# Decoder step on one core: norm factors spread inside the second product, second weight sum one block later, activations last in a step, smaller first transfers

## The chip, the core and the metric

The kernel runs on one core of a Trainium2 chip. The metric is device microseconds (us) of one execution. The engines of the core work side by side, each through its own list of instructions in order: TensorE (PE, matrix products, results in PSUM), VectorE (DVE), ScalarE (ACT), GpSimd (POOL), and SyncE (SP), which here mostly issues DMA transfers. An engine waits at an instruction until the semaphores that it names have come, and everything behind that instruction on the same engine waits too.

## What is computed

One layer of a decoder over T = 576 token columns (512 of a prompt, 64 of eight running sequences), model width 1024. The part that the change touches is the pair of half-step feed-forward networks and the norms around them:

```
def _rmsnorm(x, g):
    y = xf * lax.rsqrt(jnp.mean(xf * xf, axis=-1, keepdims=True) + EPS)
    return (y * g.astype(jnp.float32)).astype(x.dtype)

def _swiglu(h, w_up, w_down):
    a, g = jnp.split(h @ w_up, 2, axis=-1)
    return (jax.nn.silu(g) * a) @ w_down

    x = x + 0.5 * _swiglu(_rmsnorm(x, W['g_ffn1'][l]), W['w_ffn1_up'][l], W['w_ffn1_down'][l])
    mix, ... = _mixer(_rmsnorm(x, W['g_mix'][l]), ...)
    x = x + mix
    x = x + 0.5 * _swiglu(_rmsnorm(x, W['g_ffn2'][l]), W['w_ffn2_up'][l], W['w_ffn2_down'][l])
y = _rmsnorm(x, W['g_final'])
```

The hidden width is 2816, that is 22 blocks ("features" f = 0 to 21) of 128. The mixer between the two networks (mLSTM and GLA, merged by gates) starts from a product of the normed input with `w_in`, taken as a list of tiles of 128 output channels.

## The kernel before

**Number format.** Every large product is made of three passes over split operands, hi·xh, hi·xl and lo·xh. For each weight ACT writes the rounded upper part (`whi`), and DVE subtracts it from the weight (`wlo`). In the same way an activation gets its `xh` and `xl`, or `mh` and `ml`. Activations stand with channels on partitions and the 576 tokens along the row, cut into two halves of 288. A matmul is 128x128 by 128x288.

**Norms.** The channel gain is multiplied in at the split. The factor of each token comes later, at the results, which are multiplied with a tile `r` of 128x576. `Norm.start` adds the squares over partitions (PE), takes the root (ACT) and the reciprocal (DVE, line 245). `Norm.finish` spreads these factors to all partitions by 4 to 8 small matmuls (line 255) and copies them to `r` (ACT). The first product of the second network and of the mixer's input runs on the unscaled input. `start` is called from inside that first product (the list `midway`), and `finish` is called behind the second product. The PSUM pool `pd` of the large products has two buffers, so the third product can start only when the first has been read out by an operation that needs `r`.

**A feed-forward network (`ffn`).** Features 0 and 1 are plain: two products of 48 matmuls each. Features 2 to 21 are made by a scheme with seven products in place of eight: the weight is cut into four quarters A11, A12, A21, A22 (128x512 each), four sums of them are built (S1 = A21 + A22 and S2 = S1 - A11 on DVE, S3 and S4 on POOL), the input has its four sums T1 to T4 (`combine`: tiles `xt`, `xth`, `xtl`), and the blocks A11, S2, A12, S3, S1, A22, S4 of 12 matmuls each run one after the other. Between the blocks of a feature stand blocks "d" of the down product of the features before. The results are put together on ACT and DVE: `s` (copy of A11's result), `U2` and `U3` (sums, in the rows `U`), then the two halves of `t` (gate) and of `h` (value), SiLU on ACT, `h·t`, and the split `mh`/`ml`.

**Order.** This stretch is in an order written out by hand. `blocks` lists all blocks. After the matmuls of a block a step is emitted: first the `prep` events (ACT, `whi` of the block four ahead), then the posts that `later(d, ...)` has put d steps ahead (the work on the results), then the other events: weight loads, weight sums, and `prep_lo` (DVE, `wlo`). A group of four features has 9 or 11 steps per feature. A PSUM tile `pd` holds A11's and then A12's result in one half, and S1's and then S4's in the other. So block S1 must wait for the DVE operation that reads A12's half for `t` (line 408), and block S4 for the one that reads S1's result into `h` (line 410).

**Start and end.** The head (lines 502 to 549) loads the first weights and inputs in pieces on SP's queue and makes the first two products together, k by k. The last norm goes by token halves. `Norm.square` puts the square of each of the eight channel tiles on ACT, POOL adds them up in `acc`, and PE adds `acc` and the last square over partitions (`packed_sum`, line 156).

Helpers hide callers in the profile: L54 is any two-operand operation, L57 one with a scalar, L66 any activation, L122 the products of `dense`, L423 all blocks of the hand-written order.

Of the kernel before, what the change touches and what calls it, by code (L numbers as in the profile page):

```python
# [9 lines left out]
F32 = mybir.dt.float32  # L10
F32R = mybir.dt.float32r
# [4 lines left out]
P = 128  # L16
# [21 lines left out]
def step_kernel(ctx: ExitStack, tc: tile.TileContext, a):  # L38
# [75 lines left out]
    def mm3(ps, w, parts, nk, hfs):  # L114

        hi, lo = w
        for k in range(nk):
            if k == nk // 2 and midway:
                midway.pop()()
            for n, (wt, xt) in enumerate(((hi, parts[k][0]), (hi, parts[k][1]), (lo, parts[k][0]))):  # L120
                for hf in hfs:
                    nc.tensor.matmul(  # L122
                        ps[:, hf, :HALF], lhsT=wt[:, k, :], rhs=xt[:, hf * HALF:(hf + 1) * HALF],
                        start=(k == 0 and n == 0), stop=(k == nk - 1 and n == 2),
                    )
# [38 lines left out]
    class Norm:  # L164
# [11 lines left out]
        def square(self, k, s=slice(0, T)):  # L176
            n = s.stop - s.start
            acc = self.acc.setdefault(s.start, [])
# [68 lines left out]
        def finish(self, keep=True):  # L247
# [3 lines left out]
            r = xs.tile([P, 4 * n], F32, name="r", tag="r", bufs=1) if keep else None  # L251
# [10 lines left out]
    def ffn(x, norm, wup, wdn, fp, after, head=None, parts=((0, 1),)):  # L262

# [13 lines left out]
        for f in range(PLAIN):  # L277
# [30 lines left out]
        NAMES = ("A11", "S2", "A12", "S3", "S1", "A22", "S4")  # L308
        XOF = {"A11": "B11", "S2": "T2", "A12": "B21", "S3": "T3", "S1": "T1", "A22": "T4", "S4": "B22"}
        first = [0] + list(range(PLAIN, NF, GRP))  # L310
        size = [PLAIN] + [GRP] * (len(first) - 1)
        blocks, at_f = [], {}
        for g in range(1, len(first)):
            last = g == len(first) - 1
            o = 0
            for j in range(size[g]):
                f = first[g] + j
                at_f[f] = len(blocks)
                blocks += [(f, n) for n in NAMES]
# [6 lines left out]
        raw, parts_of, posts = {}, {}, {}  # L326
        pair = [None]
        tick = [0]

        def prep(i):  # L330

            b = blocks[i]
            if i % 2 == 0:
                pair[0] = [wp.tile([P, KT, P], F32R, name=f"w{n}", tag=f"w{n}", bufs=3) for n in ("hi", "lo")]
            if b[0] == "d":
                n = size[b[1]]
                src = raw["d"][b[1:]]
            else:
                n = 4
                src = raw[b[0]][b[1]]  # L340
            hi, lo = (t[:, 4 * (i % 2):4 * (i % 2) + n, :] for t in pair[0])
            act(hi, src, AF.Copy)
            parts_of[i] = hi, lo, src

        def prep_lo(i):
            hi, lo, src = parts_of[i]
            tt(lo, src, hi, ALU.subtract)
            parts_of[i] = hi, lo

        def load_up(f):  # L350
            st = wp.tile([P, 2, 4, P], F32, name="wst", tag="wst", bufs=3)
            su = fp.tile([P, 2, 4, P], F32, name="wsu", tag="wsu", bufs=2)
            for i, t in ((1, su), (0, st)):
                nc.sync.dma_start(out=t, in_=wup[f, :, i].rearrange("p (h k) c -> p h k c", h=2))
            raw[f] = {"A11": st[:, 0], "A12": st[:, 1], "A21": su[:, 0], "A22": su[:, 1]}

        def load_down(i):

            raw.setdefault("d", {})
            st = wp.tile([P, KT, P], F32, name="wst", tag="wst", bufs=3)  # L360
            _, g, o, hfs = blocks[i]
            n = size[g]
            sv_ = st[:, :2 * n, :].rearrange("p (o k) c -> p o k c", o=2)
            nc.sync.dma_start(out=sv_, in_=wdn[o:o + 2, :, first[g]:first[g] + n].rearrange("o p k c -> p o k c"))
            for u in range(2):
                raw["d"][(g, o + u, hfs)] = sv_[:, u]

        def sums(f, *names):
            w = raw[f]
            for n in names:  # L370
                a, b, op, eng = {"S1": ("A21", "A22", ALU.add, None), "S2": ("S1", "A11", ALU.subtract, None),
                                 "S3": ("A11", "A21", ALU.subtract, nc.gpsimd),
                                 "S4": ("A12", "S2", ALU.subtract, nc.gpsimd)}[n]
                w[n] = fp.tile([P, 4, P], F32, name=n, tag=n, bufs=1)
                tt(w[n], w[a], w[b], op, eng=eng)

        events = {}

        def on(i, fn, *a_):
            events.setdefault(i, []).append((fn, a_))  # L380

        for f, i in at_f.items():
            on(i - 11, load_up, f)
            on(i - 5, sums, f, "S1", "S2")
            on(i - 4, sums, f, "S3")
            on(i - 2, sums, f, "S4")
        for i, b in enumerate(blocks):
            if b[0] == "d" and b[2] % 2 == 0:
                on(i - 8, load_down, i)
            on(i - 4, prep, i)  # L390
            on(i - 4, prep_lo, i)

        def later(d, fn):
            posts.setdefault(tick[0] + d, []).append(fn)

        def seven(f, psum, lastf):
# [3 lines left out]
            s1, U2, U3 = (fp.tile([P, HALF], F32, name=n, tag=n, bufs=1) for n in ("s1", "U2", "U3"))  # L400
            t1, t2, h1, h2, r2 = t[:, :HALF], t[:, HALF:], h[:, :HALF], h[:, HALF:], r[:, HALF:]
# [4 lines left out]
            later(1, lambda: act(s1, psum["A11"], AF.Copy))  # L406
            later(2, lambda: tt(U2, psum["S2"], s1, ALU.add))
            later(3, lambda: tt(t1, psum["A11"], r[:, :HALF], ALU.mult))
            later(4, lambda: tt(U3, psum["S3"], U2, ALU.add))
            later(5, lambda: tt(h2, psum["S1"], U3, ALU.add))  # L410
            later(6, lambda: tt(h1, psum["A22"], U3, ALU.add))
            later(7, lambda: tt(t2, psum["S1"], U2, ALU.add))
            later(7, lambda: tt(t2, t2, r2, ALU.mult, eng=pool_))
# [6 lines left out]
        def run(i, work):  # L420

            for m in work:
                nc.tensor.matmul(m[0], lhsT=m[1], rhs=m[2], start=m[3], stop=m[4], skip_group_check=m[5])  # L423
            do = events.pop(i, ())
            for fn, a_ in do:
                if fn is prep:
                    fn(*a_)
            for fn in posts.pop(tick[0], ()):
                fn()
            for fn, a_ in do:  # L430
                if fn is not prep:
                    fn(*a_)
            tick[0] += 1

        with tc.manual_schedule():
            for i in range(min(events), 0):
                for fn, a_ in events.pop(i, ()):
                    fn(*a_)
            psum = {}
            for i, b in enumerate(blocks):  # L440
                if b[0] == "d":
                    _, g, o, hfs = b
                    n = size[g]
                    hi, lo = parts_of.pop(i)
                    ps = pd.tile([P, 2, 512], F32, name="pd", tag="pd")
                    work = [(ps[:, hf, :HALF], wt[:, k, :], xt[:, hf * HALF:(hf + 1) * HALF],
                             k == 0 and m == 0, k == n - 1 and m == 2, False)
                            for k in range(n) for m, (wt, xt) in enumerate(
                                ((hi, mids[g][k][0]), (hi, mids[g][k][1]), (lo, mids[g][k][0]))) for hf in hfs]
                    half = 12 if len(work) > 12 else len(work)  # L450
                    run(i, work[:half])
                    if midway:
                        midway.pop()()
                    if work[half:]:
                        run(i, work[half:])

                    def done(ps=ps, o=o, hfs=hfs, fin=g == len(first) - 1):
                        s_ = slice(hfs[0], hfs[-1] + 1)
                        stt(halves(x[o])[:, s_], ps[:, s_, :HALF], 0.5, ALU.mult, halves(x[o])[:, s_], ALU.add)
                        if fin:  # L460
                            later(1, lambda: after(o, hfs))
                    later(0, done)
                    continue
                f, n = b
                if n == "A11":
                    if (f - PLAIN) % GRP == 0:
                        mids.append([])
# [877 lines left out]
```

## Time and profile before

| | |
|---|---|
| median of 3 runs | 1604.49 us (1599.73 to 1606.45) |
| profiled execution | 1603.93 us, of which the span from first to last instruction is 1602.1 us |
| PE busy | 1563.5 us, 98% |
| DVE busy | 1061.5 us, 66% |
| ACT busy | 678.4 us, 42% |
| POOL busy | 310.0 us, 19% |
| DMA | 166.01 MB, mean 104 GB/s |
| mean granted TensorE clock | 0.996 |

The busy times are shares of one execution. A PE at 98% can get shorter only by the time in which it stands still or runs at the lower of its two clock levels, or by fewer matmuls. In rows of the trace, the first number is the start in us from the span's start, the second the duration. A bracket at the end is the idle time of that engine just before the row, and what ended it.

### The profile page before, as it was taken

What the parts mean: (1) busy time and instruction counts of PE and PEld (TensorE: products, weight loads), DVE (VectorE), ACT (ScalarE), POOL (GpSimd) and SP (SyncE); (2) the same over time, 40 slices, a digit from 0 to 9 for tenths busy, and PEclk for the clock granted to TensorE, in tenths of its full rate; (3) what the DMA queues carried; (4) which work ended last, traced back from release to release, by engine and by line L of the source; (5) the groups of instructions that cost most, each with busy time, mean ns of one, the idle gap of its engine ahead of it and who ended that gap; (6) DMA issues with size and microseconds to landing.
All of it is one profiled execution on the core that took longest, in us unless ns stands there. A gap on an engine that the chain in (4) does not pass through costs nothing.

```text
span 1602.1 us, 31170 instructions
## 1 busy us (share of the span) xinstructions
PE 1563.5 (98%) x13028; PEld 1514.5 (95%) x13028; DVE 1061.5 (66%) x1785; ACT 678.4 (42%) x1147; POOL 310.0 (19%) x300
## 2 busy tenths in 40 slices
PE   8999999999999999999999999999999999999997
PEld 7999999999998989999998989999999999999997
DVE  7986776767587666653565756633567977677775
ACT  8433433333555453631334344531453433333334
POOL 1333223321200000000100001003223422322223
PEclk9999999999999999999999999999999999999999
DMA  5222332233513313323432334442222232223223
GB/s 188 82 96 80 94 93 91 80 92 95 189 54 123 110 48 116 112 94 114 129 136 90 132 108 153 152 158 79 80 93 66 83 102 93 79 81 105 93 66 112
DMA packets 59332, 166.01 MB, mean 104 GB/s; under 512 B 6072, under 2 KB 14008, under 8 KB 58168
## 3 DMA queue, kind: packets, MB, share of 16 engines
q1 hardware_dynamic: 58616, 163.43, 31.8%
q8 instruction: 103, 1.69, 0.4%
q10 hardware_dynamic: 576, 0.59, 0.1%
q14 instruction: 37, 0.30, 0.1%
HBM read 142.60 MB, written 21.38 MB: 102 GB/s over the span
## 4 chain that ended last, share of the span: by engine, by line
PE 87%; DVE 6%; ACT 3%; issue 2%; POOL 1%; DMA 0%; SPq 0%; ACTq 0%; DVEq 0%; POOLq 0%
PE pd L122 36%; PE pd L423 32%; PE pm L423 10%; ACT whi L66 1%; DVE wlo L54 1%; PE pm L1075 1%; PE pm L794 1%; PE pd L533 1%; PE pm L1089 1%; PE pm L869 1%; DVE xt L57 1%; DVE ml L54 1%; PE pm L1141 1%; PE pm L722 1%; DVE xtl L54 0%
## 5 line engine op out<-in xcount | busy, mean ns | idle before, releaser
L66 ACT ACTIVATE whi<-wst 128x512 fp32r<-128x512 f32 (+3 forms) x301 | 217.9, 736 | 448.0 <-PE pd L122 271.8
L54 DVE TENSOR_TENSOR wlo<-wst,whi 128x512 fp32r<-128x512 f32 (+3 forms) x301 | 262.0, 871 | 22.4 <-ACT whi L66 15.1
L122 PE MATMUL pd<-xh,whi 128*128 128x288 f32 x1136 | 249.2, 298 | 5.4 <-DVE t L54 3.5
L122 PE MATMUL pd<-xh,wlo 128*128 128x288 f32 x1136 | 247.6, 296 | 0.0
L122 PE MATMUL pd<-xl,whi 128*128 128x288 f32 x1136 | 247.4, 297 | 0.0
L122 PEld LDWEIGHTS pd<-xh,whi 128*128 128x128 f32 x1136 | 182.8, 188 | 10.4 <-issue 9.7
L54 POOL TENSOR_TENSOR t<-t,r 128x288 f32<-128x288 f32 (+1 forms) x80 | 105.2, 1315 | 445.6 <-DVE t L54 399.6
L66 ACT ACTIVATE whi<-S 128x512 fp32r<-128x512 f32 x160 | 99.7, 626 | 208.9 <-PE pd L423 74.8
L122 PEld LDWEIGHTS pd<-xh,wlo 128*128 128x128 f32 x1136 | 183.5, 189 | 1.9 <-issue 1.8
L122 PEld LDWEIGHTS pd<-xl,whi 128*128 128x128 f32 x1136 | 182.6, 188 | 1.4 <-issue 1.0
L57 DVE SCALAR_TENSOR_TENSOR x<-pd,x 128x576 f32<-128x576 f32 (+1 forms) x112 | 79.8, 713 | 142.9 <-PE pd L423 116.8
L423 PE MATMUL pd<-mh,whi 128*128 128x288 f32 x704 | 156.3, 296 | 0.3 <-DVE x L57 0.3
L423 PE MATMUL pd<-mh,wlo 128*128 128x288 f32 x704 | 155.9, 296 | 0.0
L423 PE MATMUL pd<-ml,whi 128*128 128x288 f32 x704 | 155.9, 296 | 0.0
L423 PE MATMUL pd<-xh,whi 128*128 128x288 f32 x480 | 144.4, 301 | 7.5 <-DVE h L54 3.0
L423 PE MATMUL pm<-xth,wlo 128*128 128x288 f32 x480 | 141.9, 296 | 0.9 <-DVE wlo L54 0.9
L423 PE MATMUL pd<-xh,wlo 128*128 128x288 f32 x480 | 142.4, 297 | 0.0
L423 PE MATMUL pd<-xl,whi 128*128 128x288 f32 x480 | 142.3, 296 | 0.0
L423 PE MATMUL pm<-xth,whi 128*128 128x288 f32 x480 | 141.9, 296 | 0.0
L423 PE MATMUL pm<-xtl,whi 128*128 128x288 f32 x480 | 141.8, 296 | 0.0
L54 DVE TENSOR_TENSOR wlo<-S,whi 128x512 fp32r<-128x512 f32 x160 | 126.5, 791 | 0.6
L423 PEld LDWEIGHTS pd<-mh,whi 128*128 128x128 f32 x704 | 114.9, 189 | 0.7 <-DVE x L57 0.5
(318 smaller groups left out, 3227.9 us busy)
## 6 DMA issues: line engine op xcount, KB each, us to landing
wst<-in_win SPq DMA_DIRECT2D x65, 512.0 KB, 3.7
wst<-in_wup SPq DMA_DIRECT2D x46, 512.0 KB, 4.8
wst<-in_wdn SPq DMA_DIRECT2D x44, 512.0 KB, 3.7
wsu<-in_wup SPq DMA_DIRECT2D x40, 512.0 KB, 4.0
C<-in_C SPq DMA_DIRECT2D x16, 514.0 KB, 5.0
out_Cs<-C SPq DMA_DIRECT2D x16, 514.0 KB, 3.1
S<-in_S SPq DMA_DIRECT2D x4, 1024.0 KB, 4.9
out_Ss<-S SPq DMA_DIRECT2D x4, 1024.0 KB, 4.1
```

The costliest lines, as they stand in the source:

```text
L54: (eng or nc.vector).tensor_tensor(out=out, in0=in0, in1=in1, op=op)
L57: nc.vector.scalar_tensor_tensor(out=out, in0=in0, scalar=s, in1=in1, op0=op0, op1=op1)
L66: nc.scalar.activation(out=out, in_=in_, func=func, **kw)
L122: nc.tensor.matmul(ps[:, hf, :HALF], lhsT=wt[:, k, :], rhs=xt[:, hf * HALF:(hf + 1) * HALF], start=(k == 0 and n == 0), stop=(k == nk - 1 ...
L423: nc.tensor.matmul(m[0], lhsT=m[1], rhs=m[2], start=m[3], stop=m[4], skip_group_check=m[5])
L533: nc.tensor.matmul(ps[i][:, hf, :HALF], lhsT=wt[:, k, :], rhs=xt[:, hf * HALF:(hf + 1) * HALF], start=(k == 0 and n == 0), stop=(k == KT - ...
L722: nc.tensor.transpose(out=pt[:, c, j * P:(j + 1) * P], in_=src[j][:, (c0 + c) * P:(c0 + c + 1) * P], identity=ident)
L794: nc.tensor.matmul(po[32 * g:32 * g + 32, :], lhsT=qpad(b_)[j], rhs=states(b_)[j], start=(v == 0 and j == 0), stop=False)
L869: nc.tensor.matmul(pl[32 * g:32 * g + 32, c, :], lhsT=kk[:, o:o + 32], rhs=qq[:, o:o + 32], start=True, stop=True)
L1075: nc.tensor.matmul(pc, lhsT=ktok[:, c, j * P:(j + 1) * P], rhs=vtok[:, c, :], start=True, stop=True)
L1089: nc.tensor.matmul(po[:, c, :], lhsT=Cc[c - 1][:, d, es], rhs=qs[d][:, c * P:(c + 1) * P], start=False, stop=(d == 1))
L1141: nc.tensor.matmul(pu, lhsT=kb[:, b_ // 4, b_ % 4, j * P:(j + 1) * P], rhs=vb[:, b_ // 4, :], start=True, stop=True)
```

## The change

Five edits, and a move of code. The hand-written pipeline goes from inside `ffn` into the functions `pipeline` and `unite` beside it, with the same blocks and the same `later` distances; the diff below leaves that move out.

```
 def mm3(ps, w, parts, nk, hfs):
             if k == nk // 2 and midway:
-                midway.pop()()
+                midway.pop(0)()
 def square(self, k, s=slice(0, T)):
+            last = KT - 1 if n == T else KT - 2
-            if k == 0 or k == KT - 1:
+            if k == 0 or k >= last:
                 acc.append(sq)
 def ffn(...):
                 if f == 0:
                     midway.append(norm.start)
                 pg = up(f, 0)
+                if f == 0:
+                    midway.append(norm.finish)
                 pa = up(f, 1)
                 if f == 0:
-                    r = norm.finish()
+                    r = norm.r
-            on(i - 5, sums, f, "S1", "S2")
-            on(i - 4, sums, f, "S3")
+                on(i - 5, sums, b[0], "S1")
+                on(i - 4, sums, b[0], "S2", "S3")
-            later(e[2], lambda: tt(h, h, t, ALU.mult))
+            later(e[2], lambda: tt(h, h, t, ALU.mult), not lastf)
             later(e[3], lambda: act(hi, h, AF.Copy))
-            later(e[3], lambda: tt(lo, h, hi, ALU.subtract))
+            later(e[3], lambda: tt(lo, h, hi, ALU.subtract), not lastf)
+        def later(d, fn, last=False):
+            posts.setdefault(tick[0] + d, []).append((last, fn))
 def run(i, work):
-            for fn in posts.pop(tick[0], ()):
-                fn()
+            late = posts.pop(tick[0], ())
+            for last, fn in late:
+                if not last:
+                    fn()
             for fn, a_ in do:
                 if fn is not prep:
                     fn(*a_)
+            for last, fn in late:
+                if last:
+                    fn()
-        load_w(0, 2)
-        load(0, 1)
-        load_w(2, 5)
+        load_w(0, 1)
+        load(0)
+        load_w(1, 3)
+        load(1)
+        load_w(3, 5)
         midway.append(n2.start)
-        first = [win_tile(), win_tile()]
-        r = n2.finish()
+        first = [win_tile()]
+        midway.append(n2.finish)
+        first.append(win_tile())
+        r = n2.r
```

Three places show how instructions move. The first is DVE in the first network, around features 5 and 6 (before, then after). `U_1246` (after: `U_1254`) is U3 of feature 5, `S_1336` and `S_1338` (after: `S_1341` and `S_1360`) are the sums S1 and S2 of feature 6, and `h<-pd` is the read of S1's result that block S4 waits for.

```order
L54 TENSOR_TENSOR h<-h,t 128x576
L54 TENSOR_TENSOR t<-pd,r 128x288
L54 TENSOR_TENSOR wlo<-wst,whi 128x512
L54 TENSOR_TENSOR ml<-h,mh 128x576
L54 TENSOR_TENSOR U_1246<-pm,U_1245 128x288
L54 TENSOR_TENSOR S_1336<-wsu 128x512
L54 TENSOR_TENSOR S_1338<-S_1336,wst 128x512
L54 TENSOR_TENSOR wlo<-wst,whi 128x512
L54 TENSOR_TENSOR h<-pd,U_1246 128x288
```

```order
L54 TENSOR_TENSOR t<-pd,r 128x288
L54 TENSOR_TENSOR wlo<-wst,whi 128x512
L54 TENSOR_TENSOR h<-h,t 128x576
L54 TENSOR_TENSOR U_1254<-pm,U_1253 128x288
L54 TENSOR_TENSOR S_1341<-wsu 128x512
L54 TENSOR_TENSOR wlo<-wst,whi 128x512
L54 TENSOR_TENSOR ml<-h,mh 128x576
L54 TENSOR_TENSOR h<-pd,U_1254 128x288
L54 TENSOR_TENSOR S_1360<-S_1341,wst 128x512
```

The split `ml` has moved from ahead of U3 to behind S1 and `wlo`, `h·t` behind `t` and `wlo`, and the sum S2 from ahead of `h<-pd` to behind it.

The second place is DVE in the second network's start, around the read of its first product into `t` (before, then after).

```order
L57 SCALAR_TENSOR_TENSOR xt<-x_11968,sm,xg 128x288
L57 SCALAR_TENSOR_TENSOR xt<-x_11968,sm,xt 128x288
L54 TENSOR_TENSOR wlo<-wst,whi 128x1024
L54 TENSOR_TENSOR xtl<-xt,xth 128x576 x2
L54 TENSOR_TENSOR t<-pd,r 128x576
L54 TENSOR_TENSOR S_13806<-wsu 128x512
```

```order
L57 SCALAR_TENSOR_TENSOR xt<-x_11974,sm,xg 128x288
L57 SCALAR_TENSOR_TENSOR xt<-x_11974,sm,xt 128x288
L54 TENSOR_TENSOR xtl<-xt,xth 128x576
L54 TENSOR_TENSOR t<-pd,r 128x576
L54 TENSOR_TENSOR xtl<-xt,xth 128x576
L54 TENSOR_TENSOR wlo<-wst,whi 128x1024
L54 TENSOR_TENSOR S_13812<-wsu 128x512
```

The read `t` now stands behind one `xtl` instead of behind `wlo` and two `xtl`.

The third place is DVE at the mixer's first tiles. `G` is the read of the first tile (gates), `Gs` its split copy that the gate products use, `kTg` the read of the third tile.

```order
L54 TENSOR_TENSOR wlo<-wst,whi 128x1024
L54 TENSOR_TENSOR G<-pd,r 128x576
L57 SCALAR_TENSOR_TENSOR qTg<-pd,r 128x576
L54 TENSOR_TENSOR Gs<-G,Gs 16x576
L54 TENSOR_TENSOR kTg<-pd,r 128x576
```

```order
L54 TENSOR_TENSOR G<-pd,r 128x576
L54 TENSOR_TENSOR Gs<-G,Gs 16x576
L57 SCALAR_TENSOR_TENSOR qTg<-pd,r 128x576
L54 TENSOR_TENSOR wlo<-wst,whi 128x1024
L54 TENSOR_TENSOR kTg<-pd,r 128x576
```

`G` now stands ahead of the `wlo` of the next tile, and `Gs` ahead of `qTg`. On PE the four spreading matmuls stand in the middle of the second tile's 48 matmuls instead of behind them.

## Rows read from the trace of the kernel before

**Rows 1.** The page, busy time of each engine.

```profile
PE 1563.5 (98%) x13028; PEld 1514.5 (95%) x13028; DVE 1061.5 (66%) x1785; ACT 678.4 (42%) x1147; POOL 310.0 (19%) x300
```

**Rows 2.** Waits of PE: line, releaser, us in total, times, longest.

```profile
PE pd L423 <- DVE h L54: 3.0, 4, 1.3
PE pd L423 <- ACT whi L66: 2.9, 4, 0.8
PE pd L423 <- DVE t L54: 2.0, 13, 0.2
```

**Rows 3.** Stretches: length, each engine's busy time, granted clock, DMA.

```profile
49.27:390.00 340.73, 336.63 (x2501) 332.74 (x2501) 254.79 (x415) 131.22 (x235) 100.78 (x75) 1.00 0.29 90
1216.88:1563.00 346.12, 341.99 (x2545) 338.11 (x2544) 258.99 (x421) 134.13 (x241) 100.89 (x75) 1.00 0.28 88
124.33:141.88 17.55, 17.55 (x134) 17.55 (x134) 13.23 (x22) 7.22 (x13) 5.18 (x4) 1.00 0.29 91
433.00:446.00 13.00, 13.00 (x96) 12.77 (x97) 2.04 (x3) 11.67 (x23) 0.00 (x0) 1.00 0.14 42
1202.94:1206.36 3.42, 3.42 (x16) 3.42 (x16) 2.86 (x3) 0.69 (x2) 2.68 (x2) 0.50 0.00 0
```

**Rows 4.** Timeline of DVE at a feature of the 11-step kind, 144 to 150 us.

```profile
144.66 0.76 DVE L54 TENSOR_TENSOR ml<-h,mh 128x576 fp32r<-128x576 f32 x1 [1.72 <-ACT mh L66]
...
146.30 0.45 DVE L54 TENSOR_TENSOR t<-pd,r 128x288 f32<-128x288 f32 x1
...
148.36 0.69 DVE L54 TENSOR_TENSOR S<-S,wst 128x512 f32<-128x512 f32 x1
```

**Rows 5.** Timeline of PE at the same place.

```profile
146.37 0.29 PE L423 MATMUL pm<-xth,wlo 128*128 128x288 f32 x1
146.81 0.40 PE L423 MATMUL pd<-xth,whi 128*128 128x288 f32 x1 [0.15 <-DVE t L54]
```

**Rows 6.** Timelines of DVE and PE between features 5 and 6.

```profile
110.94 0.76 DVE L54 TENSOR_TENSOR ml<-h,mh 128x576 fp32r<-128x576 f32 x1 [0.64 <-ACT mh L66]
...
113.91 0.45 DVE L54 TENSOR_TENSOR h<-pd,U 128x288 f32<-128x288 f32 x1
...
114.51 0.37 PE L423 MATMUL pd<-xh,whi 128*128 128x288 f32 x1 [1.30 <-DVE h L54]
```

**Rows 7.** Timelines of PE and DVE at the mixer's first tiles.

```profile
429.94 1.14 PE L255 MATMUL pm<-v,cst 128*128 128x144 f32 x8
433.00 0.50 PE L122 MATMUL pd<-xh,whi 128*128 128x288 f32 x2 [1.92 <-DVE G L54]
...
432.11 0.75 DVE L54 TENSOR_TENSOR G<-pd,r 128x576 f32<-128x576 f32 x1
```

**Rows 8.** Timelines of PE and DVE at the second network's start.

```profile
1202.42 0.50 PE L122 MATMUL pd<-xh,whi 128*128 128x288 f32 x2 [3.49 <-DVE t L54]
...
1199.06 1.21 DVE L54 TENSOR_TENSOR wlo<-wst,whi 128x1024 fp32r<-128x1024 f32 x1
...
1201.53 0.74 DVE L54 TENSOR_TENSOR t<-pd,r 128x576 f32<-128x576 f32 x1
```

**Rows 9.** Timelines of ACT, POOL and PE at the end.

```profile
1591.40 0.44 ACT L66 ACTIVATE sq<-x 128x288 f32<-128x288 f32 x1 [1.15 <-DVE x L57]
...
1592.02 0.79 POOL L54 TENSOR_TENSOR acc<-acc,sq 128x288 f32<-128x288 f32 x1
...
1592.86 0.36 PE L156 MATMUL pm<-acc,cst 128*32 128x72 f32 x8 [2.05 <-POOL acc L54]
```

**Rows 10.** Timeline of PE, its first matmuls.

```profile
6.58 1.09 PE L533 MATMUL pd<-xh,whi 128*128 128x288 f32 x3 [6.58 <-ACT xh L66]
```

**Rows 11.** Timelines of DVE and POOL where both run, and POOL's pause.

```profile
105.05 1.92 DVE L54 TENSOR_TENSOR wlo<-wsu,whi 128x512 fp32r<-128x512 f32 x1
...
104.52 1.89 POOL L54 TENSOR_TENSOR t<-t,r 128x576 f32<-128x576 f32 x1 [1.22 <-ACT t L66]
...
152.56 1.19 POOL L54 TENSOR_TENSOR t<-t,r 128x288 f32<-128x288 f32 x1 [12.29 <-DVE t L54]
```

More of the change, by code (lines that the diff above doesn't have):

```diff
@@ L250, in finish @@
             per = 2 if n == T // 4 else 4
-            r = xs.tile([P, 4 * n], F32, name="r", tag="r", bufs=1) if keep else None
+            self.r = r = xs.tile([P, 4 * n], F32, name="r", tag="r", bufs=1) if keep else None
             for i in range(4 // per):
@@ L260, in finish, with unite @@
             return r
+    NAMES = ("A11", "S2", "A12", "S3", "S1", "A22", "S4")
+    XOF = {"A11": "B11", "S2": "T2", "A12": "B21", "S3": "T3", "S1": "T1", "A22": "T4", "S4": "B22"}
+    def unite(psum, t, h, r, fp, later):
+        s1, U2, U3 = (fp.tile([P, HALF], F32, name=n, tag=n, bufs=1) for n in ("s1", "U2", "U3"))
+        later(1, lambda: act(s1, psum["A11"], AF.Copy))
+        later(2, lambda: tt(U2, psum["S2"], s1, ALU.add))
+        later(3, lambda: tt(t[:, :HALF], psum["A11"], r[:, :HALF], ALU.mult))
+        later(4, lambda: tt(U3, psum["S3"], U2, ALU.add))
+        later(5, lambda: tt(h[:, HALF:], psum["S1"], U3, ALU.add))
+        later(6, lambda: tt(h[:, :HALF], psum["A22"], U3, ALU.add))
+        later(7, lambda: tt(t[:, HALF:], psum["S1"], U2, ALU.add))
@@ L304, in ffn @@
             mids[0].append((hi, lo))
-        NAMES = ("A11", "S2", "A12", "S3", "S1", "A22", "S4")
-        XOF = {"A11": "B11", "S2": "T2", "A12": "B21", "S3": "T3", "S1": "T1", "A22": "T4", "S4": "B22"}
         first = [0] + list(range(PLAIN, NF, GRP))
         size = [PLAIN] + [GRP] * (len(first) - 1)
-        blocks, at_f = [], {}
+        blocks = []
         for g in range(1, len(first)):
@@ L316, in ffn @@
             for j in range(size[g]):
-                f = first[g] + j
-                at_f[f] = len(blocks)
-                blocks += [(f, n) for n in NAMES]
+                blocks += [(first[g] + j, n) for n in NAMES]
                 for _ in range(1 if last and j >= GRP - 2 else 2):
@@ L324, in ffn @@
         blocks += [("d", len(first) - 1, o, hfs) for hfs in parts for o in range(KT)]
[L326 to L383, printed above, removed]
-            on(i - 5, sums, f, "S1", "S2")
-            on(i - 4, sums, f, "S3")
[L386 to L394, printed above, removed]
@@ L396, in seven, with up_done @@
-        def seven(f, psum, lastf):
+        def up_done(f, psum, later):
+            if (f - PLAIN) % GRP == 0:
+                mids.append([])
             t = fp.tile([P, T], F32, name="t", tag="t", bufs=2)
             h = fp.tile([P, T], F32, name="h", tag="h", bufs=2)
-            s1, U2, U3 = (fp.tile([P, HALF], F32, name=n, tag=n, bufs=1) for n in ("s1", "U2", "U3"))
-            t1, t2, h1, h2, r2 = t[:, :HALF], t[:, HALF:], h[:, :HALF], h[:, HALF:], r[:, HALF:]
+            lastf = f == NF - 1
@@ L405, in seven @@
             e = (8, 9, 9, 10) if lastf else (9, 9, 12, 13)
[L406 to L412, printed above, removed]
@@ L413, in seven @@
-            later(7, lambda: tt(t2, t2, r2, ALU.mult, eng=pool_))
+            unite(psum, t, h, r, fp, later)
+            later(7, lambda: tt(t[:, HALF:], t[:, HALF:], r[:, HALF:], ALU.mult, eng=pool_))
             later(e[0], lambda: act(t, t, AF.Silu))
             later(e[1], lambda: tt(t, t, r, ALU.mult, eng=pool_))
-            later(e[2], lambda: tt(h, h, t, ALU.mult))
+            later(e[2], lambda: tt(h, h, t, ALU.mult), not lastf)
             later(e[3], lambda: act(hi, h, AF.Copy))
-            later(e[3], lambda: tt(lo, h, hi, ALU.subtract))
@@ L420, in run @@
[L420 to L427, printed above, removed]
-            for fn in posts.pop(tick[0], ()):
-                fn()
[L430 to L467, printed above, removed]
-                    pair_ = pd.tile([P, 2, 512], F32, name="pd", tag="pd")
-                    psum = {"A11": pair_[:, 0, :HALF], "S1": pair_[:, 1, :HALF]}
-                    psum["A12"], psum["S4"] = psum["A11"], psum["S1"]
-                    seven(f, psum, f == NF - 1)
-                if n not in psum:
-                    psum[n] = bank([P, HALF], "b" + n)
-                hi, lo = parts_of.pop(i)
-                go_on = n in ("A12", "S4")
-                run(i, [(psum[n], wt[:, k, :], xt, not go_on and k == 0 and m == 0, k == 3 and m == 2, go_on)
-                        for k, (xh, xl) in enumerate(norm.block(XOF[n]))
-                        for m, (wt, xt) in enumerate(((hi, xh), (hi, xl), (lo, xh)))])
-            while posts:
-                for fn in posts.pop(min(posts)):
-                    fn()
@@ new lines, in up_done, with down_work @@
+            later(e[3], lambda: tt(lo, h, hi, ALU.subtract), not lastf)
+        def down_work(b, w, ps):
+            _, g, o, hfs = b
+            n = size[g]
+            hi, lo = w
+            return [(ps[:, hf, :HALF], wt[:, k, :], xt[:, hf * HALF:(hf + 1) * HALF],
+                     k == 0 and m == 0, k == n - 1 and m == 2, False)
+                    for k in range(n) for m, (wt, xt) in enumerate(
+                        ((hi, mids[g][k][0]), (hi, mids[g][k][1]), (lo, mids[g][k][0]))) for hf in hfs]
@@ new lines, in down_done @@
+        def down_done(b, ps, later):
+            _, g, o, hfs = b
+            s_ = slice(hfs[0], hfs[-1] + 1)
+            stt(halves(x[o])[:, s_], ps[:, s_, :HALF], 0.5, ALU.mult, halves(x[o])[:, s_], ALU.add)
+            if g == len(first) - 1:
+                later(1, lambda: after(o, hfs))
+        pipeline(blocks, norm, fp, lambda f, i: wup[f, :, i], up_done,
+                 (lambda b: size[b[1]], lambda b: wdn[b[2]:b[2] + 2, :, first[b[1]]:first[b[1]] + size[b[1]]],
+                  down_work, down_done))
```

100 lines of the change are left out of this document (added).

## The prediction

> **What bounds the kernel now.** I read the busy times first. PE is busy 1563.5 us, 98% of the span, and no other engine more than two thirds [rows 1]. So the end is set by PE, and this change, which takes no product away, can only win the places where PE stands still or runs at the lower clock level. The view of PE's waits says where these are inside the hand-written order: 4 waits for `h`, 4 that are put down to `whi`, 13 short ones for `t`, 7.9 us in all [rows 2]. Then I looked at stretches. Between 124.33 and 141.88 PE runs without a stop: two of the 134 matmuls there belong to the piece before, and 132 in 17.55 us make 0.133 us from start to start. With this pace the first network's 2501 matmuls would take 332.6 us and the second's 2545 would take 338.5, but the stretches last 340.73 and 346.12 [rows 3]. So about 8 us in each are lost. The timelines of DVE and PE beside each other say why, and I come to that with the edits. Outside the two networks there are three larger stops: 1.92 us at the mixer's first tiles [rows 7], 3.49 us at the second network's start, where the granted clock was 0.50 (1.2 of 2.4 GHz) for 3.42 us afterwards [rows 3, 8], and 2.05 us at the end [rows 9].
>
> **Activations last, S2 later.** In the 11-step features DVE reaches `ml` and stands 1.72 us for ACT's `mh`; U2, a `wlo` and the read `t` are queued behind it, and `t` ends at 146.75 [rows 4]. Block S1 waits for this `t` because it writes over the PSUM half that `t` reads. PE's matmul of 146.37 would have had a successor at 146.50. It came at 146.81 [rows 5]. After the change the order is U2, `wlo`, `ml`, `t` (the row order for this place differs from before only by `ml`'s move). U2 and `wlo` take 146.30 - 144.66 less `ml`'s own 0.68, that is 0.96 us, and now fit into the 1.72 us in which DVE stood. So `t` ends near 145.8, 0.7 us ahead of need, and this stop goes.
>
> At features 5 and 6 the stop is the read `h<-pd` for block S4. It begins at 113.91, with `ml` (0.64 us of waiting), U3, S1, S2 and a `wlo` in front [rows 6]. After the change S2 (about 0.65 of DVE's time) stands behind it, and U3 starts where the 0.64 us of waiting were, while `ml` itself stays in front. So `h<-pd` comes 0.64 + 0.65 = 1.3 us earlier, against 1.30 us of PE's idle time [rows 6]; I leave 0.2 us there. The four waits of 0.6 to 0.8 us put down to `whi` are the same thing: the `whi` named is of a block four ahead, and the same DVE chain stands in front of the same read. They have 1.3 - 0.8 = 0.5 us to spare.
>
> A stop costs more than its idle time. At 146.81 the row gives 0.15 us, but from start to start 0.44 went by instead of 0.133, and the next matmul's duration is 0.40 instead of 0.30 [rows 5]. I take 0.27 us more for each, so 21 stops cost 7.9 + 21 x 0.27 = 13.6 us of the 15.7 lost. Two leftovers of 0.2 away, the gain is **13.2 us**. Bounds: if the stops only shrink by half, 6.6; if all the lost time comes back, 15.7.
>
> S2 later must not become a stop of its own. It is 0.69 us of DVE [rows 4] and then needs `whi` and `wlo`, some 2 us, and its block is five blocks (5 x 12 x 0.133 = 8 us) away. If this cover were gone, each us would count forty times. POOL's S4 needs S2 as well; it is emitted two blocks later and is used still later.
>
> What is moved on DVE could meet POOL. At 105.05 a `wlo` beside a POOL operation takes 1.92 us [rows 11], and other 128x512 operations on DVE take 0.69 [rows 4]. S2's new place in the 11-step features is about 150 us, and POOL has a pause of 12.29 us until 152.56 [rows 11], so I add nothing. The Trainium skill (SBUF — State Buffer, "Who interferes with whom") says that a DVE operation with two inputs in SBUF contends with a GpSimd one that reads SBUF, since they share a port pair. By that rule, an S2 laid beside a POOL sum would cost more than in its old place; these two rows agree on the size of the effect, and POOL's pause says that it isn't met here.
>
> **Factors inside the second product, mixer.** Before, the spreading matmuls begin at 429.94, `G` ends at 432.86 and PE starts the third tile at 433.00 [rows 7]. After, they stand 24 matmuls (3.2 us) earlier, so `G` ends at 429.7 at the latest, ahead of the second tile's end at 431.1. What is late next is `Gs`: the gate products now stand ahead of the third tile, and a copy on ACT and a subtraction on DVE after `G`, some 0.7 us each by the 0.75 of `G`, put them at 431.2 to 431.5. So of 1.92 + 0.27 some 0.3 stays. I take **2.0 us** (1.0 to 3.0; the upper end if the gate chain, which starts earlier, shortens a later wait too).
>
> **The same, second network.** `t` is held up by DVE, not by the factors: it is queued behind `wlo` (1.13 until the next start) and two `xtl` [rows 8]. After, `wlo` and one `xtl` stand behind it. (1201.53 - 1199.06 - 1.13) / 2 = 0.67 is one `xtl`, so `t` comes 1.8 us earlier and PE starts near 1200.6. That alone gives 1.8 us. The clock is the other part. At 0.50 for 3.42 us, half of that, 1.7 us, is lost. The stop would still be 1.7 us long; it then resembles the one of 1.92 us at 433.00, behind which the granted clock stayed 1.00 [rows 3, 7], so I take the drop as gone: **3.5 us** (1.8 to 3.7).
>
> The first network's start keeps its stops: there the factors come from the head and DVE's list is about as long as before. I take 0.1, between -0.8 and 1.8.
>
> **Last squares to PE.** PE's last sum waits for POOL's `acc`, 1592.02 + 0.79. Without that addition it waits for the last square, done at 1591.84, so 1.0 us earlier [rows 9]; 8 more small matmuls cost at most the 0.36 of a group of 8, nearer 0.15. **0.8 us** (0.6 to 1.0).
>
> **Smaller first transfers.** PE's first matmul at 6.58 waits for `xh` [rows 10], which waits for a transfer behind 256 KB of weights. 128 KB of these move behind it; at the mean 104 GB/s of the whole run that would be 1.2 us, an upper bound. The lower bound is a loss of 0.5, since x1 now has two more issues ahead of it on SP's queue. Nothing shows a 64 KB weight transfer here; I take **0.3**. The Trainium skill (DMA: Bandwidth & Descriptors, "Rules for kernel authors") speaks against this edit: small transfers should be joined, under 64 KB one pays mostly overhead. By it the gain would be about nothing, 0.3 us less in the sum; no run here shows it yet.
>
> **The sum.** 13.2 + 2.0 + 3.5 + 0.1 + 0.8 + 0.3 = 19.9 us off the profiled execution's 1603.93: 1584.0. The median of the runs is 1604.49, 0.6 above it, and the runs lie 7 us apart, so I predict **1584 us**. About 0.5%, 8 us, is what a measurement of this kernel can tell from no change.
>
> **Rivals.** *(a) The stops only shrink.* DVE is two thirds busy, and a little collision with POOL (1.2 us, [rows 11]) at a feature is more than the 0.5 to 0.7 us of slack. If half the 13.6 us stay, the time is 1584.0 + 6.6 = 1590.6, and 1594 with the clock drop of the second network and the weaker ends of the seams (1.7 + 1.0 + 0.3). *(b) The reordering does nothing:* something else, such as ACT's `mh`, holds the same reads; only seams and tail win: 1603.93 - 6.7 = 1597.2. Against it speaks that DVE stood idle ahead of `ml` while U2's inputs were there. *(c) More comes back:* all the 15.7 us, the first network's clock drop and the upper bounds of the seams: 1584.0 - 2.5 - 1.7 - 1.2 = 1578.6. *(d) Slower:* S2's later place meets POOL or the later `ml` delays the down products; one collision on PE's path costs 1.92 - 0.69 = 1.2 us, in each of 40 features 49 us: 1584 + 49 = 1633. It decides from 0.7 us a feature on (28 us, over the 19.9 won plus 8). Against it speak POOL's pause and 8 us of cover.
>
> **How the numbers follow.** Forecast, 1580 to 1588: 0.55; (a), up to 1594: 0.20; (b): 0.09, of which 0.07 within 0.5% and 0.02 just faster; (c): 0.10; (d): 0.06, half of it beyond 0.5% slower and half eaten up within 0.5%. Faster by over 0.5% is below 1596.5: 0.55 + 0.20 + 0.10 + 0.02 = 0.87; same 0.10; slower 0.03. The range leaves out (b), (d) and the last of (c): 1577 to 1594.
>
> **What would show it.** Right: no `t` and `whi` waits of PE under L356 (the blocks' new line), the stretch of the second network's blocks near 339 us, `ml` behind U2 without 1.72 us of idle time in front of it, clock 1.00 behind the second network's start, PE's last sum starting right after the last square. Wrong: new waits of PE for S2's `whi`, for `mh` or `ml` in "d" blocks, DVE operations of 1.3 to 1.9 us beside POOL in places where they were 0.69, or a 0.50 stretch that remains. It would make the prediction wrong above all if `h<-pd` and `t` come late for another reason than `ml` and S2.

## The result, and the profile after

The changed kernel takes 1581.24 us (median of 4 runs, 1580.12 to 1582.0), the kernel before 1604.92 in the same comparison: a ratio of 0.9858, 95% interval 0.9834 to 0.9881. It is faster by 23.7 us; 1584 was forecast, 20 us of gain. The profiled execution has a span of 1578.3 us, 23.8 less than before.

PE's busy time and its waits on the page and in the view of waits, the longest waits first:

```profile
PE 1552.6 (98%) x13044; PEld 1510.5 (96%) x13044; DVE 1060.1 (67%) x1787; ACT 682.4 (43%) x1149; POOL 307.8 (20%) x298
...
PE pd L558 <- ACT xh L66: 6.0, 1, 6.0
PE pm L356 <- DVE wlo L54: 1.8, 1, 1.8
PE pm L749 <- DVE vTg L54: 1.5, 1, 1.5
PE pm L896 <- issue: 1.4, 1, 1.4
PE pd L122 <- DVE t L54: 1.4, 1, 1.4
...
PE pd L356 <- DVE t L54: 0.8, 1, 0.8
...
PE pd L356 <- ACT s L66: 0.6, 1, 0.6
PE pm L256 <- DVE v L212: 0.6, 1, 0.6
PE pm L156 <- POOL acc L54: 0.5, 1, 0.5
```

L356 is now the line of the blocks. The lists of 4, 4 and 13 waits [rows 2] are gone: the one wait for `t` and the ones for `wlo` and `s` all lie at the first network's start, between 43 and 50 us. PE's busy time fell by 11 us although it runs 16 matmuls more, since matmuls right behind a stop, and those at the half clock, are counted with longer durations (0.40 us in place of 0.30 at 146.81, [rows 5]; 0.44 at the half clock behind 45.65 us of the kernel before).

The two stretches of blocks, and two where the clock had been half (length, busy times, granted clock, DMA):

```profile
50.00:382.00 332.00, 331.93 (x2497) 331.73 (x2498) 254.09 (x414) 132.08 (x235) 100.82 (x75) 1.00 0.29 91
1201.96:1539.85 337.89, 337.82 (x2546) 337.61 (x2545) 258.92 (x421) 136.06 (x242) 100.85 (x75) 1.00 0.29 91
45.00:50.00 5.00, 3.56 (x26) 3.23 (x25) 5.00 (x9) 2.37 (x6) 2.23 (x1) 1.00 0.16 52
1189.00:1195.00 6.00, 5.84 (x44) 5.84 (x45) 5.97 (x7) 3.07 (x4) 3.27 (x2) 1.00 0.15 44
```

The second network's 2544 block matmuls take 337.89 us, 0.1328 each; before, from the same matmul's start to the same matmul's start, it was 346.37.

Where the 23.8 us of the profiled executions came from, read at the starts of the same matmuls of both traces (the 49th block matmul, the first network's last block matmul, the first matmul of the mixer's 11th tile, and so on):

| stretch | before | after | gain | forecast |
|---|---|---|---|---|
| start to 49th block matmul (head and first network's start) | 50.46 | 49.98 | 0.5 | 0.4 |
| from there to the first network's last block matmul | 365.80 | 357.42 | 8.4 | 6.6 |
| to the mixer's 11th tile | 88.77 | 86.49 | 2.3 | 2.0 |
| mixer, to four tiles before its end of dense work | 679.22 | 679.22 | 0.0 | 0 |
| to the second network's first block matmul | 32.47 | 28.85 | 3.6 | 3.5 |
| its blocks up to the 2545th | 346.37 | 337.89 | 8.5 | 6.6 |
| last blocks and last norm | 39.06 | 38.48 | 0.6 | 0.8 |

DVE and PE of the changed kernel at the 11-step feature that [rows 4, 5] show before:

```profile
139.83 0.46 DVE L54 TENSOR_TENSOR U<-pm,s 128x288 f32<-128x288 f32 x1 [0.62 <-issue]
140.35 0.69 DVE L54 TENSOR_TENSOR wlo<-S,whi 128x512 fp32r<-128x512 f32 x1
140.97 0.75 DVE L54 TENSOR_TENSOR ml<-h,mh 128x576 fp32r<-128x576 f32 x1
141.63 0.45 DVE L54 TENSOR_TENSOR t<-pd,r 128x288 f32<-128x288 f32 x1
...
142.63 0.29 PE L356 MATMUL pm<-xth,wlo 128*128 128x288 f32 x1
142.76 0.29 PE L356 MATMUL pd<-xth,whi 128*128 128x288 f32 x1
```

`ml` has no wait in front of it any more, since U2 and `wlo` run while ACT makes `mh`. `t` ends at 142.08, and block S1 begins at 142.76 in step with the matmul before it: 0.7 us of slack, as forecast.

Between features 5 and 6 [rows 6], DVE's list ends as follows:

```profile
109.52 0.75 DVE L54 TENSOR_TENSOR ml<-h,mh 128x576 fp32r<-128x576 f32 x1
110.19 0.45 DVE L54 TENSOR_TENSOR h<-pd,U 128x288 f32<-128x288 f32 x1
110.56 0.67 DVE L54 TENSOR_TENSOR S<-S,wst 128x512 f32<-128x512 f32 x1
```

`h<-pd` ends at 110.64 and PE's block S4 starts at 110.78, where 110.55 would have been in step: 0.23 us are left of 1.46. This is the one stop left in each network's blocks.

### The profile page after: what moved, and what is told of

It is laid out like the page before. It is cut to its first block, busy times and chain, and to the rows that moved or that the text cites. A ratio compares the mean times of both kernels' runs of the same rounds, so it can differ in the third digit from the quotient of the medians.

```text
span 1578.3 us, 31282 instructions
## 1 busy us (share of the span) xinstructions
PE 1552.6 (98%) x13044; PEld 1510.5 (96%) x13044; DVE 1060.1 (67%) x1787; ACT 682.4 (43%) x1149; POOL 307.8 (20%) x298
## 4 chain that ended last, share of the span: by engine, by line
PE 90%; DVE 4%; ACT 2%; issue 1%; POOL 1%; DVEq 0%; POOLq 0%; ACTq 0%
PE pd L122 36%; PE pd L356 34%; PE pm L356 12%; PE pm L1102 1%; PE pm L821 1%; DVE wlo L54 1%; PE pm L1116 1%; PE pm L896 1%; PE pm L1168 1%; PE pm L749 1%; PE pm L938 0%; PE pm L609 0%; PE pm L156 0%; PE pm L1114 0%; PE pm L922 0%
## 5 line engine op out<-in xcount | busy, mean ns | idle before, releaser
L356 PE MATMUL pd<-mh,whi 128*128 128x288 f32 x704 | 156.1, 296 | 0.0
L356 PE MATMUL pd<-mh,wlo 128*128 128x288 f32 x704 | 155.9, 296 | 0.0
L356 PE MATMUL pd<-ml,whi 128*128 128x288 f32 x704 | 155.8, 296 | 0.0
L356 PE MATMUL pm<-xth,wlo 128*128 128x288 f32 x480 | 141.8, 295 | 1.8 <-DVE wlo L54 1.8
L356 PE MATMUL pd<-xh,whi 128*128 128x288 f32 x480 | 142.1, 296 | 0.7 <-ACT s L66 0.6
L356 PE MATMUL pd<-xh,wlo 128*128 128x288 f32 x480 | 142.0, 296 | 0.0
L356 PE MATMUL pm<-xtl,whi 128*128 128x288 f32 x480 | 141.6, 295 | 0.0
L356 PE MATMUL pm<-xth,whi 128*128 128x288 f32 x480 | 141.6, 295 | 0.0
L356 PE MATMUL pd<-xl,whi 128*128 128x288 f32 x480 | 141.2, 294 | 0.0
L356 PEld LDWEIGHTS pd<-mh,whi 128*128 128x128 f32 x704 | 114.9, 189 | 0.2
```

## The experiments

All times are medians of 4 to 6 runs; the kernel before took 1602.7 to 1603.7 us beside them, 1 to 2 us less than the 1604.92 beside the changed kernel, so a us or two of the 23.7 may be noise. The rows of the runs are quoted where a verdict rests on them.

**The two posts back at their place in the step (no_last).**

```
-later(e[2], lambda: tt(h, h, t, ALU.mult), not lastf)
+later(e[2], lambda: tt(h, h, t, ALU.mult))
-later(e[3], lambda: tt(lo, h, hi, ALU.subtract), not lastf)
+later(e[3], lambda: tt(lo, h, hi, ALU.subtract))
```

> The changed kernel with h*t and ml back at their old place in a step, S2 still one block later. Theory (DVE's list: ml and S2 both stand in front of the reads that blocks S1 and S4 wait for): the seven stops per network in the 11-step features come back, 0.42 us each from start to start, and parts of the longer ones (the 0.64 us of waiting for mh, not S2's 0.65): about 4.4 us per network, 8.8 in all, 1590 us. Rival (S2's place alone made the gain): within 1.5 us of the changed kernel's 1581.2. Rival (neither, the gain came with weights or POOL): also 1581.

Measured: 1589.16 us (ratio to before 0.9917, 0.9902 to 0.9932), 7.9 above the changed kernel. The waits for the two reads are back in its view of waits:

```profile
PE pd L356 <- DVE t L54: 2.1, 14, 0.2
...
PE pd L356 <- DVE h L54: 1.6, 4, 0.6
```

The stretches of blocks got 4.5 and 4.6 us longer, where 4.4 each was expected. The profiled execution also had the half clock for 6.83 us at the first network's start.

**S2 back five blocks ahead (no_s2).**

```
-on(i - 5, sums, b[0], "S1")
-on(i - 4, sums, b[0], "S2", "S3")
+on(i - 5, sums, b[0], "S1", "S2")
+on(i - 4, sums, b[0], "S3")
```

> The changed kernel with S2 back five blocks ahead, h*t and ml still last in a step. Theory: no stop in the 11-step features; in the 9-step features S2 stands again in front of the read for block S4, but the wait for mh doesn't, so some 0.3 us at two features and 0.9 at the one with the longest stop: 1.4 us per network, 2.8 in all, 1584 us. Rival (S2's place made the gain): 16 us back, 1597 us.

Measured: 1585.15 us (0.989, 0.9876 to 0.9905), 3.9 above. The stretches of blocks are 2.2 and 2.5 us longer; I had expected 1.4. The view of waits has no wait for `t` in the long features and

```profile
PE pd L356 <- DVE h L54: 2.8, 8, 0.8
```

8 waits, where I had counted on 6: at the other 9-step features (67.96 and 97.54 us, 0.33 us each) S2 alone makes `h<-pd` late too. S2's place is worth something, but the rival that it made the whole gain falls.

**Both undone (no_last_s2).** The edits of the two runs above together.

> Both undone: the blocks' order is that of before, the other edits stay. Theory: all of the 16.9 us that the two networks' blocks gained come back, 1598 us, which is more than the two single ones together (11.6), since each alone leaves slack that the other would need. If the two were independent: 1593 us. Rival (the blocks' gain came from another edit, such as factors or transfers): 1581 to 1585 us.

Measured: 1597.76 us (0.9968, 0.9955 to 0.998), 16.5 above. The blocks are 8.4 and 8.5 us longer, as long as before, while the two single runs give 7.9 + 3.9 = 11.8. So each edit alone keeps part of the slack that the other needs, and the sum of the single undoings understates the pair by 4.7 us, and by 3.1 in the stretches of blocks alone.

**Only ml last (ml_only), only h·t last (ht_only).** One of the two lines of no_last each: in ml_only the first, in ht_only the second.

> The changed kernel with h*t back among the posts, ahead of the weight work of its step; only ml stays last. Theory (what counts is that ml's wait for mh doesn't stand in front of U2, U3 and the two reads; h*t only changes places with operations that end before the same read): within 1.5 us of the changed kernel, 1581 to 1583 us, no stop in the 11-step features. Rival (h*t beside POOL's work is what mattered): stops come back, 1585 us or more.

> The changed kernel with ml back among the posts; only h*t stays last. Theory (ml's wait for mh is the cause): the stops in the 11-step features are back, and since mh now comes no earlier, as with both posts undone or worse: 1589 us or more. Rival (h*t's place does it): 1581 us.

Measured: ml_only 1580.4 us (0.9858, 0.9838 to 0.9878), the same as the changed kernel, its blocks' stretches 0.20 and 0.24 us longer; ht_only 1595.66 us (0.9946, 0.9931 to 0.9961), 14.4 above it, and 6.5 worse than no_last, which has both posts back. DVE of ht_only at a long feature, and its longest waits of PE in the blocks:

```profile
144.16 0.76 DVE L54 TENSOR_TENSOR ml<-h,mh 128x576 fp32r<-128x576 f32 x1 [1.73 <-ACT mh L66]
...
PE pd L356 <- DVE h L54: 4.8, 6, 1.4
PE pd L356 <- DVE t L54: 2.1, 14, 0.2
```

The 1.73 us in front of `ml` are those of before. In the short features, `h·t` later makes `mh` later, and a `ml` that is still early waits for it: 0.75 us at each, where no_last has 0.65 to 0.70 at some and none at 95.20. The longest stop for `h` is 1.4 us, 0.6 in no_last. So of the two "last" posts `ml` carries all of the gain, and `h·t` is harmless only because `ml` is behind it.

**The factors behind the second product again (no_finish).**

```
-                if f == 0:
-                    midway.append(norm.finish)
                 pa = up(f, 1)
                 if f == 0:
-                    r = norm.r
+                    r = norm.finish()
-        first = [win_tile()]
-        midway.append(n2.finish)
-        first.append(win_tile())
-        r = n2.r
+        first = [win_tile(), win_tile()]
+        r = n2.finish()
```

> The changed kernel with the factors spread behind the second product again, in the mixer and in the second network. Theory: 2.3 us back at the mixer's first tiles and 3.6 at the second network's start, of which 1.7 by a stretch of 3.4 us at a granted clock of 0.50 that comes back with the stop of 3.5 us: 1587 us. Rival (the lower clock there isn't tied to the stop's length): the clock stays 1.00 and it is 1585.4, or the changed kernel's own 1.4 us stop would show it in other executions too.

Measured: 1586.91 us (0.9902, 0.9887 to 0.9916), 5.7 above. PE's stop at the second network's start, and the stretch behind it:

```profile
1195.64 0.50 PE L122 MATMUL pd<-xh,whi 128*128 128x288 f32 x2 [3.36 <-DVE t L54]
...
1195.80:1199.50 3.70, 3.70 (x18) 3.70 (x18) 3.17 (x4) 1.04 (x2) 2.60 (x2) 0.54 0.01 3
```

The stop and the low clock came back together, as expected. At the mixer the 11th tile starts 3.8 us later than in the changed kernel, counted from the last block. 2.3 of that are the order's, as expected: the kernel before comes there 2.3 us later. The other 1.5 go with a half clock of 3.41 us behind the mixer's second stop, which neither the kernel before nor the changed kernel has in its trace.

**The blocks' order alone (blocks_only).** Of the change only the two edits inside the blocks; factors, last squares and first transfers are as before.

> Of the changed kernel only the order inside the blocks (S2 one block later, h*t and ml last); factors, last squares and first transfers as before. Theory (the edits lie at separate places and add up): 16.9 us below the kernel before, 1586 to 1587 us against its 1603.5 or so, with the stops of 1.92 and 3.49 us and the 0.50 stretch at the second network's start back. Rival (the edits overlap): clearly more than 17 us of gain or less than 15.

Measured: 1587.39 us against 1603.65 (0.9897, 0.988 to 0.9913), 16.3 of gain; in its trace the two stretches of blocks are 8.4 and 8.5 us shorter than before, as in the changed kernel. With the 5.0 us that the other edits gained by themselves (no_last_s2) that makes 21.3 of the 23.7, so the edits add up to within 2.4 us. But one part of the expectation failed, the clock:

```profile
1193.40 0.51 PE L122 MATMUL pd<-xh,whi 128*128 128x288 f32 x2 [3.24 <-DVE t L54]
...
1191.66:1197.00 5.34, 3.60 (x27) 3.63 (x28) 5.08 (x7) 2.28 (x3) 2.35 (x2) 1.00 0.16 49
```

With a stop of 3.24 us the granted clock stayed 1.00. The three other executions took 1.5 to 2.0 us longer at a mean clock of 0.995 in place of 0.996, as one more stretch at the half clock would make them; where it lay is not on record.

**Head and tail undone (no_head_tail).**

```
-            last = KT - 1 if n == T else KT - 2
+            last = KT - 1
-        load_w(0, 1)
-        load(0)
-        load_w(1, 3)
-        load(1)
-        load_w(3, 5)
+        load_w(0, 2)
+        load(0, 1)
+        load_w(2, 5)
```

> The changed kernel with the first transfers in their old sizes and order, and only the last square straight to PE's sum in the last norm. The two places don't meet, so their stretches are read apart. Theory: PE's first matmul 0.5 us later, but the first block of the hand-written order at the same time as in the changed kernel, since there PE waits for the reciprocal of the first norm, which comes no earlier; at the end 0.5 to 0.6 us more between the last block and the end. In all 1581.2 + 0.6 = 1581.8 us. Rival (the head's 0.5 us count): first block 0.5 us later, 1582.3 us. Rival (the Trainium skill's rule that joined transfers are better): PE's first matmul earlier than 6.01.

Measured: 1581.59 us (0.9866, 0.9851 to 0.9881), no difference that the runs tell. In the trace PE's first matmul is at 6.82 in place of 6.01, so the smaller transfers and their new order do start PE 0.8 us earlier, but the first block of the hand-written order is at 39.87 in place of 39.72. PE of the changed kernel, in the head's end:

```profile
29.38 1.25 PE L256 MATMUL pm<-v,cst 128*128 128x144 f32 x8 [0.58 <-DVE v L212]
```

It waits for the reciprocal, a stop that the kernel before doesn't have. The tail: from the last block to the root of the norm 2.9 us with POOL's addition, 2.3 in the changed kernel.

**A step further (plain_dve, early_t).** The first takes `t·r` of the plain features to DVE; the second adds that the read into `t` is written ahead of `combine`.

```
 # plain_dve
-            tt(t, t, r, ALU.mult, eng=nc.gpsimd)
+            tt(t, t, r, ALU.mult)
 # early_t, in addition
-            if f == 0:
-                for q in range(4):
-                    norm.combine(q, fp)
             t = fp.tile([P, T], F32, name="t", tag="t", bufs=2)
             tt(halves(t), pg, halves(r), ALU.mult)
+            if f == 0:
+                for q in range(4):
+                    norm.combine(q, fp)
```

> The changed kernel with the plain features' t*r on DVE instead of POOL. Theory (at the first network's start DVE stands 2.57 us for POOL's t, and h, ml and the weights for block S2 come late by that): the three stops there, 1.76, 0.60 and 0.83 us, shrink to about 1 us together, 2.5 us gained, 1578.7 us; the second network's start is unchanged or 0.2 better. Rival (DVE is the bound there, the work only moves): 1581 us, or later by the two operations of 0.75 us.

> As the run with t*r on DVE, and the read of the first plain product into t written ahead of the combinations of the input, so that DVE reaches it sooner. Theory: at the second network's start r has been there for 3 us when DVE comes to t, so the stop of 1.37 us goes, with its restart 1.6 us; the first network's start as in the run before. 1577.1 us. Rival (t's place only moves the wait to the next reader, or T1 to T4 come late for the first blocks): 1578.7 us or more.

Measured: plain_dve 1577.41 us (0.9841, 0.9826 to 0.9856), early_t 1576.06 (0.9831, 0.9816 to 0.9846), 5.2 below the changed kernel and the fastest of all. What they are after is DVE's wait for POOL's `t` at the first network's start, here in the changed kernel:

```profile
40.90 1.95 DVE L54 TENSOR_TENSOR h<-raw,t 128x576 f32<-128x576 f32 x1 [2.57 <-POOL t L54]
```

In plain_dve the stop for `wlo` there is 0.35 in place of 1.76 us, the 0.60 one is gone, but the one for `t` grew from 0.83:

```profile
42.02 0.40 PE L356 MATMUL pm<-xth,wlo 128*128 128x288 f32 x1 [0.35 <-DVE wlo L54]
...
48.20 0.40 PE L356 MATMUL pd<-xth,whi 128*128 128x288 f32 x1 [1.05 <-DVE t L54]
```

So 1.8 us came of the 2.5 expected. The mixer was 1.2 us shorter besides, in early_t too: PE's pause of 1.4 us at L896, for which the profile shows no releaser, is missing in both. It stands with 1.1 or 1.4 us in the traces of the ten other kernels, and the edits don't touch that place. Why these two lack it is not shown, so 1.2 us of what they gained is not explained by the stops. In early_t the stop at the second network's start is gone (from there to its first block 1.7 us less than in plain_dve):

```profile
1182.50 0.75 DVE L54 TENSOR_TENSOR t<-pd,r 128x576 f32<-128x576 f32 x1
```

`t` is read at 1182.50, while PE is still in the second product.

## Why the prediction was right, and where a size was off

**The mechanism in the blocks** was right, step by step: `ml` waiting for `mh` in front of U2 and `t` in the long features (no_last, ml_only, ht_only), S2 and that wait together in front of `h<-pd` in the short ones (no_s2, no_last_s2). The cover that was claimed for a later S2 held: no wait of PE for S2's weights appears.

**The mis-sized term** is the 13.2 us for the blocks; it measured 16.9. The step "21 stops cost 7.9 + 21 x 0.27" took the stops from the view of waits. From the starts of PE's matmuls there are 21 stops in each network, 42 in all, half of them too short to be listed there; they cost 8.7 us per network over the pace of 0.1328, of which 0.3 is left in each. One of the unlisted ones, in the kernel before, takes 0.33 us from start to start in place of 0.133, and its row has no bracket:

```profile
67.85 0.29 PE L423 MATMUL pm<-xth,wlo 128*128 128x288 f32 x1
68.18 0.37 PE L423 MATMUL pd<-xh,whi 128*128 128x288 f32 x1
```

All 42 together cost 17.4 us before. So the 0.27 for each listed stop was about right, and their number was wrong: the unlisted ones make the 3.7 us that the forecast lacks. The way by the stretches, which gave 15.7 us of lost time as an upper bound, was nearer, and still below what came. It fell short because the counts of matmuls in a stretch include those that only reach into it, and because the pace was rounded up to 0.133.

**The factors in the mixer** (2.0 forecast, 2.3 measured) went as said, only that nothing of the stop is left, where 0.3 was expected. This is how it looks after (there are eight spreading matmuls, not four as said under the change):

```profile
417.92 1.14 PE L256 MATMUL pm<-v,cst 128*128 128x144 f32 x8
...
422.07 0.69 PE L650 MATMUL pm<-Gs,w2s 128*128 128x288 f32 x4
...
419.54 0.76 DVE L54 TENSOR_TENSOR G<-pd,r 128x576 f32<-128x576 f32 x1 [1.22 <-ACT r L66]
```

`G` ends at 420.30, 1.8 us ahead of the gate products at the second tile's end, `Gs` at 421.81, 0.26 ahead, and PE goes on with them without a listed wait. The stop and its restart gave 2.1 us; the later wait for `vTg` is 1.5 in place of 1.6.

**The second network's start** (3.5 forecast, 3.6 measured) keeps a stop, 1.4 us where 1.7 was forecast:

```profile
1188.37 0.74 DVE L54 TENSOR_TENSOR t<-pd,r 128x576 f32<-128x576 f32 x1
...
1189.16 0.53 PE L122 MATMUL pd<-xh,whi 128*128 128x288 f32 x2 [1.37 <-DVE t L54]
```

The queue's part, 1.8 us, is shown: blocks_only, with the old order there and the clock at 1.00, is 1.8 us longer in this stretch than the changed kernel. The clock's part, 1.7 us, came out in this execution. That the shorter stop is the reason is supported and not shown: in the traces of the eight kernels with a stop of 1.4 to 1.7 us here the clock stayed 1.00, and with stops of 3.49 and 3.36 us it fell, but with 3.24 it didn't. So what the kernel before loses by the clock here is 0 or 1.7 us from one execution to the next, and that it was 1.7 in the trace compared was in part luck.

**Head and first network's start** (0.4 forecast, 0.5 measured) came out by other ways than said. The transfers' 0.6 us at the first matmul are lost at the reciprocal: the first block starts at 39.72, before at 39.75. The gain lies behind it, and is the clock's: the half clock of 3.4 us of before was absent in this execution, by luck, for in eight of the ten other kernels run here it was there. From the first to the 49th block matmul the changed kernel takes 10.26 us, the kernel before 10.71, and the seven others with one such stretch 10.5 to 10.8. So the half clock costs 0.2 to 0.5 us there and not half its length, 1.7. PE without it is sooner at the read `t` and stands 0.83 us for it, a stop that the kernel before does not have there:

```profile
49.98 0.40 PE L356 MATMUL pd<-xth,whi 128*128 128x288 f32 x1 [0.83 <-DVE t L54]
```

With this wait the listed stops come to 3.2 us, before to 2.3. With the 64 KB transfers, and the first piece of x ahead of 128 KB of weights, the first matmul started 0.6 us earlier than before and 0.8 earlier than in no_head_tail; size and order are not told apart by any run. The rule of the Trainium skill (DMA: Bandwidth & Descriptors, "Rules for kernel authors") that small transfers should be joined would not have given that. For the time as a whole nothing was gained, which is what the prediction made of that rule, but by another cause.

**The tail** gave 0.6 of 0.8:

```profile
1568.12 0.31 PE L156 MATMUL pm<-acc,cst 128*32 128x72 f32 x2 [0.54 <-POOL acc L54]
...
1568.16 0.44 ACT L66 ACTIVATE sq<-x 128x288 f32<-128x288 f32 x1 [1.15 <-DVE x L57]
1569.58 0.32 ACT L66 ACTIVATE v<-pm,cst 128x72 f32<-128x72 f32 x1 [0.97 <-PE pm L156]
```

From the sum's start to the root it now takes 1.46 us, before 0.6 behind the start of [rows 9]: the sum begins ahead of the last square, waits for it inside (it ends at 1568.60), and then has 20 of its 24 matmuls left. So the square, not POOL, is the last to come, as said; the 0.15 for the added matmuls was too little. Before, the root (ACT's `v`) starts 0.62 us behind the end of POOL's `acc`; now it starts 0.98 us behind the end of the square.

**The rivals.** (a), (b) and (d) did not happen: no DVE operation in S2's new place was longer than 0.69 us, except one at the second network's start, where POOL runs beside it:

```profile
1191.55 1.81 DVE L54 TENSOR_TENSOR S<-S,wst 128x512 f32<-128x512 f32 x1
...
1190.84 1.97 POOL L54 TENSOR_TENSOR t<-t,r 128x576 f32<-128x576 f32 x1 [16.42 <-ACT t L66]
```

The price is as bounded, 1.1 us, and PE didn't wait for it. This agrees with what the Trainium skill (SBUF — State Buffer, "Who interferes with whom") says of DVE and GpSimd. Rival (c) came nearest: all the lost time in the blocks came back but 0.6 us.

## What to carry to other kernels

Where an engine works through a list in order, look at what stands in front of each operation that frees a PSUM buffer: one that waits for another engine and that nobody needs soon, like `ml` here, belongs behind the reads that PE waits for. Count stops from the starts of PE's matmuls, not from the list of waits, and undo edits in pairs as well as singly, since two edits that give slack to the same deadline don't add. And take an operation off the queue of a slow helper at a seam where the other engine stands idle: DVE waited 2.6 us there for POOL.

## What the hardware showed beside that

The clock at a seam is a matter of the single execution. At the first network's start a stop of 1.8 us, with one of 0.6 us or less behind it, was followed by a granted clock of 1.00 in the changed kernel, by 0.50 for 3.41 us in no_s2, no_last_s2 and no_finish, and by 0.50 for 6.83 us in no_last. At the mixer's stop for `vTg`, 1.5 to 1.6 us in all twelve traces, 0.50 for 3.41 us appeared in no_finish alone. In the last norm the 8 small matmuls took 1.11 us in the changed kernel and 1.88 and 1.94 in no_head_tail and early_t, where the half clock had begun by then. Of the seven executions of the kernel before beside plain_dve the one with a mean clock of 0.993 took 1607.96 us, the one with 0.998 took 1602.05. So a difference of 2 to 4 us between two single traces needs no edit behind it.
